# Attention products of a hybrid block: plain fp32 products rewritten as three passes over rounded halves

## The chip, the cores and the metric

The kernel runs on one core of one Trainium2 chip. The metric is the device time of one execution in microseconds (us), and the kernel before takes 2869.97 us, the median of 3 runs (2869.61 to 2870.84). Engines are named as in the profile: PE is TensorE with its weight loads PEld, DVE is VectorE, ACT is ScalarE, POOL is GpSimd, SP issues most DMAs.

## The reference

One recurrent and attention block is followed by two further layers, all on 256 tokens of width 2048 in fp32. What matters here are the three kinds of attention. Each head multiplies queries by keys (scores) and weights by values (weighted sums):

```python
# first block: 16 heads, "stick breaking", strictly causal
z = einsum('bhqd,bhkd->bhqk', qb, kb) * scale
w = where(causal, exp(log_sigmoid(z) + excl), 0.0)   # excl: suffix sums of log_sigmoid(-z)
out = einsum('bhqk,bhkd->bhqd', w, vb)
# two layers, 4 differential heads: two softmaxes over half the head width each
s = einsum('bqhcd,bkhcd->bhcqk', qi, k) * scale + bias
a = p[:, :, 0] - lam * p[:, :, 1];  out = einsum('bhqk,bkhd->bqhd', a, v)
# two layers, 8 dilated heads: a softmax over scores with bias, then the weighted sum
```

The rest are projections by large weight matrices (7852 blocks of 128x128, streamed from memory), a recurrence, a convolution of 31 taps in each of the two layers, norms and a feed-forward stage.

## The kernel before

Activations lie transposed, features on the 128 partitions and 256 tokens along the columns. Weights come in slabs of 8 blocks (`prep`, L196): a DMA brings `raw`, ACT writes the rounded high half `whi` (type fp32r), DVE writes the low half `wlo = raw - whi`. Four slabs are prepared ahead (`LA`). An activation is kept as a high and a low half side by side in one tile of 512 columns (`split`, L308). A projection (`proj`) runs, per block, a pass of the high weights over both halves (512 columns, L217) and a pass of the low weights over the high half (256 columns, L218). Where the output is narrower, `mm3` runs three passes of 256 columns (L220 to L222). Values are made by `vproj` with the tokens on the partitions.

The attention products were left as plain fp32 products: one of 256 columns and one of 128 columns for each score tile and for each weighted sum, since the upper right of the causal square is left out. Scores of the first block stand at L598 and L599, its weighted sums at L619 and L620. For both layers the scores stand at L795 and L796 (`scores`) and the weighted sums at L819 and L820 (`weighted`). The suffix sums of the first block are already products of halves with triangles and columns of minus one (`sum2`, L573 and L574).

PE runs in the order in which the program is written (`manual_schedule`). The attention steps are closures in a queue, `sides`: `interleave` cuts each head into stages, two steps apart, and `side()` runs one step behind every projection, or behind every fourth block in `vproj`. So the work of a head fills the gaps of the next projections. The instructions of ACT, DVE, POOL and SP are put in order by a list scheduler that goes by the program's order, moved up where `tc.high_priority()` stands. Each engine then runs its list strictly in order. The convolution taps (`tap`, L909, 31 for each of 4 column groups and each layer) run on DVE in the same stretch as the differential heads; `bg(n)` places them.

A softmax for the layers (`softmax`, `scale_rows`) is a chain on DVE, ACT and DVE: scores plus bias, row maximum, exponential with sum, reciprocal, scaling (L778 to L791). `transposed` sends its result through PE (L810 to L812) and ACT copies it out of PSUM. Tiles come from fixed sets: 51 slots `c` of 512 columns, 14 slots `w` of 384 columns, 4 PSUM tiles `pm`, 2 `pa` and 2 `pst`.

Of the kernel before, what the change touches and what calls it, by code (L numbers as in the profile page):

```python
# [13 lines left out]
OP = mybir.AluOpType  # L14
# [62 lines left out]
def hybrid_kernel(ctx, tc, wst, xin, pin, vec, cst, relb, onehot, out, order):  # L77
# [203 lines left out]
    def vproj(key, mc, ops, scale_cols, sides_between=True):  # L281
        os = [pm(512) for _ in range(2)]
        for kr, a in enumerate(ops):
            ah, al = hl(a)
            wh, wl = wnext(key, kr, mc, 4)
            first, last = kr == 0, kr == len(ops) - 1
            for b, o in enumerate(os):
                tb = slice(b * 128, (b + 1) * 128)
                PE.matmul(o, ah[:, tb], wh, start=first, stop=False)  # L289
                PE.matmul(o, ah[:, tb], wl, start=False, stop=False)  # L290
                PE.matmul(o, al[:, tb], wh, start=False, stop=last)  # L291
            if sides_between and kr % 4 == 3:
                side()
        v = []
        for b, o in enumerate(os):
            t = slot()
            if scale_cols is None:
                act(t, o, AF.Copy)
            else:
                act(t, o, AF.Copy, scale=scale_cols[:, b:b + 1])  # L300
            v.append([t[:, j * 128:(j + 1) * 128] for j in range(4)])
        return v

    def split(src):
# [271 lines left out]
    def head_job(col, gcol):  # L576
        o = proj("w_in", col, ops)
        q = joined(o, "qk", R)
        s = ct()
        with tc.high_priority():  # L580
            act(s, q, AF.Square)
            s = pool_split(s, *hl(slot(F32R)))

        def fin():
            p = pst()
            sum2(p[:, :256], ones1r, s)
            r = rsqrt(p[:, :256], EPS, ct(), ct())
            V.scalar_tensor_tensor(q, q, gcol, r, op0=OP.mult, op1=OP.mult)
        return q, fin

    yo = {}

    def stick_stages(h, q, k, v0, v1):
        d = {}

        def s1():
            p = pa()
            PE.matmul(p[:, 0:256], k[:, 0:128], q, start=True, stop=True)  # L598
            PE.matmul(p[:, 256:384], k[:, 128:256], q[:, 128:256], start=True, stop=True)  # L599
            z, t = wt(), wt()  # L600
            V.tensor_tensor(z, p[:, :384], maskneg, op=OP.add)
            act(t, z, AF.Abs)
            act(t, t, AF.Exp, scale=-1.0)
            act(t, t, AF.Ln, bias=one)
            V.scalar_tensor_tensor(t, z, 0.0, t, op0=OP.max, op1=OP.add)
            d["z"], d["t"] = z, pool_split(t, wt(384, F32R), wt(384, F32R))

        def s2():
            p = pa()
            t, z = d["t"], d["z"]  # L610
            sum2(p[:, 0:384], negtrir, t, last=False)
            sum2(p[:, 128:256], negonesr, [a[:, 256:384] for a in t], first=False)
            V.tensor_tensor(z, p[:, :384], z, op=OP.add)
            act(z, z, AF.Exp)

        def s3():
            p = pa()
            w = d["z"]
            PE.matmul(p[:, 0:256], v0, w[:, 0:256], start=True, stop=False)  # L619
            PE.matmul(p[:, 128:256], v1, w[:, 256:384], start=False, stop=True)  # L620
            yo[h] = split(p[:, 0:256])
            d.clear()
        return s1, s2, s3
# [168 lines left out]

    def scores(q, k):
        p = pa()
        PE.matmul(p[:, 0:256], q[:, 128:256], k, start=True, stop=True)  # L795
        PE.matmul(p[:, 256:384], q[:, 0:128], k[:, 0:128], start=True, stop=True)  # L796
        return p

    def apart(t):
        w = slot()  # L800
        a, b = hl(w)
        nc.gpsimd.memset(a[64:128], 0.0)
        nc.gpsimd.memset(b[0:64], 0.0)
        act(a[0:64], t[0:64], AF.Copy)
        act(b[64:128], t[64:128], AF.Copy)
        return w

    def transposed(s):
        p = pa()
        PE.transpose(p[:, 0:128], s[:, 256:384], ident)  # L810
        PE.transpose(p[:, 128:256], s[:, 0:128], ident)
        PE.transpose(p[:, 256:384], s[:, 128:256], ident)  # L812
        w = wt()
        act(w, p[:, :384], AF.Copy)
        return w

    def weighted(w, v0, v1):
        p = pa()
        PE.matmul(p[:, 0:256], v0, w[:, 0:256], start=True, stop=False)  # L819
        PE.matmul(p[:, 128:256], v1, w[:, 256:384], start=False, stop=True)  # L820
        return p[:, 0:256]

    def dil_stages(h, q, k, v0, v1, res):
# [16 lines left out]
    def diff_stages(h, q, k, v0, v1, nlam, gcol, res):  # L840
        d = {}

        def s1():
            d["a"], l = softmax(scores(q[:, 0:256], k), h, 64.0 ** -0.5)
            scale_rows(d["a"], l)

        def s1b():
            s, l = softmax(scores(q[:, 256:512], k), h, 64.0 ** -0.5)
            a = d["a"]
            V.tensor_tensor(l, l, nlam.to_broadcast([128, 2]), op=OP.mult)  # L850
            V.scalar_tensor_tensor(a[:, 0:256], s[:, 0:256], l[:, 0:1], a[:, 0:256], op0=OP.mult, op1=OP.add)
            V.scalar_tensor_tensor(a[:, 256:384], s[:, 256:384], l[:, 1:2], a[:, 256:384], op0=OP.mult, op1=OP.add)

        def s2():
            d["w"] = transposed(d.pop("a"))

        def s3():
            o = weighted(d.pop("w"), v0, v1)
            t, s = ct("resa"), ct()
            act(t, o, AF.Copy)  # L860
            act(s, o, AF.Square)
            d["t"], d["s"] = t, pool_split(s, *hl(slot(F32R)))

        def s4():
            t = d.pop("t")
            p = pst()
            sum2(p[:, :256], ones1r, d.pop("s"))
            r = rsqrt(p[:, :256], EPS_2, ct(), ct())
            V.scalar_tensor_tensor(t, t, gcol, r, op0=OP.mult, op1=OP.mult)
            res[h] = t  # L870
        return s1, s1b, s2, s3, s4

    for layer in range(DEPTH_2):
# [65 lines left out]
        def plain(col, key):  # L939
            return joined(proj(W, col, ops), key)  # L940

        aq, ak = [], []
        for lst, col in ((aq, C2_AQ), (ak, C2_AK)):
            for j in range(A_H):
                if layer and lst is aq:
                    t, b = folded(proj(W, col + j, dgs, cols=258), "aqk")
                    act(t, t, AF.Identity, bias=b)
                else:
                    t = plain(col + j, "aqk")
                lst.append(apart(t) if lst is aq else t)  # L950
                bg(4)
        if layer:
            del dgs
# [31 lines left out]
        for g in range(2):  # L985
            bq, bk = [], []
            for lst, col in ((bq, C2_BQ), (bk, C2_BK)):
                for j in range(4):
                    lst.append(plain(col + 4 * g + j, "bqk"))
                    bg(5 if g == 0 else 4)  # L990
                    side()
            bv = vproj(W, C2_BV + 4 * g, ops, None)
# [279 lines left out]
```

## Time and profile before

| what | us |
|---|---|
| median of 3 runs | 2869.97 |
| the profiled execution, its own time | 2869.06 |
| span of the profile, first to last instruction | 2866.9 |
| PE busy | 2846.1 (99%) |
| DVE busy | 2018.1 (70%) |
| ACT busy | 1645.0 (57%) |
| POOL busy | 136.8 (5%) |

The profiled execution took 0.91 us less than the median. The TensorE clock was granted in full (0.998 over the run). The lengths of matmuls in the profile overlap, since they are pipelined, so the cost of one is read from the distance between starts. On DVE, too, one instruction starts a little before the one ahead of it ends. A plain fp32 product appears as two matmul records and two weight loads, a product of rounded halves as one of each.

### The profile page before, as it was taken

Reading aid. Unit: us, or ns where it says so; the run is one execution under the profiler, and the core shown is the slowest. Engines: PE = TensorE matmul, PEld = TensorE weight load, DVE = VectorE, ACT = ScalarE, POOL = GpSimd, SP = SyncE. Lnnn points to the kernel's source line nnn. Section 1 sums busy time; section 2 is a strip of 40 time slices with the busy share of each in tenths; the row PEclk is TensorE's granted clock in tenths of the full one; section 3 lists DMA queues with packets and bytes.
Section 4 is the critical chain, followed back from the end, with each engine's and each line's share of the span. In section 5 each row is a group of like instructions: output and inputs, shape, how many; then the busy total and the mean of one; then the engine's idle time right before and its main releaser. Section 6 shows DMA issues by size and latency. Waiting matters only on the chain.

```text
span 2866.9 us, 43239 instructions
## 1 busy us (share of the span) xinstructions
PE 2846.1 (99%) x16414; PEld 2496.8 (87%) x16414; DVE 2018.1 (70%) x3306; ACT 1645.0 (57%) x2628; POOL 136.8 (5%) x155
## 2 busy tenths in 40 slices
PE   9999999999999999999999999999999999999997
PEld 8988888888888888888888888888888889888886
DVE  8788765666665776566565666776795688896676
ACT  6778764677765555544445455555464656554654
POOL 0112100111110000000000000000000001000000
PEclk9999999999999999999999999999999999999999
DMA  7565555545455556555555555655555555545553
GB/s 250 179 199 180 196 190 185 184 165 166 163 175 180 188 191 217 188 187 191 186 189 189 190 190 185 211 186 191 177 169 169 176 189 173 193 158 176 170 185 124
DMA packets 146433, 527.04 MB, mean 184 GB/s; under 512 B 16708, under 2 KB 17244, under 8 KB 146224
## 3 DMA queue, kind: packets, MB, share of 16 engines
q1 hardware_dynamic: 144720, 520.00, 54.8%
q0 software_dynamic: 1504, 4.29, 0.4%
q8 instruction: 128, 2.10, 0.3%
q14 instruction: 81, 0.66, 0.1%
HBM read 522.10 MB, written 4.47 MB: 184 GB/s over the span
## 4 chain that ended last, share of the span: by engine, by line
PE 99%; DVE 1%; DMA 0%; ACT 0%; SPq 0%; issue 0%; DVEq 0%
PE pm L217 55%; PE pm L218 28%; PE pm L290 3%; PE pm L289 3%; PE pm L291 3%; PE pm L221 2%; PE pm L220 2%; PE pm L222 2%; PE pa L795 0%; PE pa L819 0%; PE pa L598 0%; PE pa L796 0%; PE pa L619 0%; DVE x L1122 0%; DMA x<-xin_dram 0%; PE pa L217 0%
## 5 line engine op out<-in xcount | busy, mean ns | idle before, releaser
L217 PE MATMUL pm<-c,whi 128*128 128x512 f32 x6778 | 2382.6, 395 | 1.6 <-DVE c L355 1.6
L218 PE MATMUL pm<-c,wlo 128*128 128x256 f32 x6778 | 1898.5, 280 | 0.1
L196 DVE TENSOR_TENSOR wlo<-raw,whi 128x1024 fp32r<-128x1024 f32 (+1 forms) x984 | 1203.8, 1224 | 783.3 <-ACT whi L98 777.4
L98 ACT ACTIVATE whi<-raw 128x1024 fp32r<-128x1024 f32 (+1 forms) x984 | 1039.4, 1057 | 967.4 <-PE pm L217 500.4
L217 PEld LDWEIGHTS pm<-c,whi 128*128 128x128 f32 x6778 | 1273.1, 188 | 294.5 <-DVE c L355 1.9
L218 PEld LDWEIGHTS pm<-c,wlo 128*128 128x128 f32 x6778 | 1275.6, 188 | 0.8 <-DVE wlo L196 0.4
L98 ACT ACTIVATE c<-pm 128x256 f32<-128x256 f32 (+1 forms) x376 | 150.5, 402 | 110.7 <-PE pm L218 106.4
L98 ACT ACTIVATE c<-c 128x256 fp32r<-128x256 f32 (+2 forms) x357 | 139.2, 408 | 46.6 <-DVE c L450 24.9
L228 DVE TENSOR_TENSOR c<-pm,c 128x256 f32<-128x256 f32 x338 | 141.1, 418 | 4.5 <-ACT c L98 4.5
L289 PE MATMUL pm<-whi,c 128*128 128x512 f32 x320 | 126.9, 396 | 0.0
L290 PE MATMUL pm<-wlo,c 128*128 128x512 f32 x320 | 126.3, 395 | 0.0
L291 PE MATMUL pm<-whi,c 128*128 128x512 f32 x320 | 126.1, 394 | 0.0
L909 DVE SCALAR_TENSOR_TENSOR c<-w,sv,c 128x256 f32<-128x256 f32 x240 | 109.4, 497 | 0.8
L221 PE MATMUL pm<-c,whi 128*128 128x256 f32 (+1 forms) x377 | 106.4, 282 | 0.0
L220 PE MATMUL pm<-c,whi 128*128 128x256 f32 (+1 forms) x377 | 106.3, 282 | 0.0
L222 PE MATMUL pm<-c,wlo 128*128 128x256 f32 (+1 forms) x377 | 106.0, 281 | 0.0
L104 ACT ACTIVATE c<-c 128x256 f32<-128x256 f32 x219 | 85.5, 407 | 16.0 <-DVE c L228 14.1
L230 DVE TENSOR_TENSOR c<-c,c 128x256 f32<-128x256 f32 x176 | 75.8, 431 | 4.2
L291 PEld LDWEIGHTS pm<-whi,c 128*128 128x128 f32 x320 | 60.1, 188 | 14.2
L289 PEld LDWEIGHTS pm<-whi,c 128*128 128x128 f32 x320 | 60.1, 188 | 13.7
L290 PEld LDWEIGHTS pm<-wlo,c 128*128 128x128 f32 x320 | 60.1, 188 | 13.5
L220 PEld LDWEIGHTS pm<-c,whi 128*128 128x128 f32 x377 | 70.9, 188 | 0.9
(245 smaller groups left out, 1570.5 us busy)
## 6 DMA issues: line engine op xcount, KB each, us to landing
raw<-wst_dram SPq DMA_DIRECT2D x980, 512.0 KB, 3.3
scratch<-rows POOLq DMA_DIRECT2D x1, 2304.0 KB, 17.7
out_dram<-x SPq DMA_DIRECT2D x8, 256.0 KB, 2.0
x<-xin_dram SPq DMA_DIRECT2D x6, 256.0 KB, 7.7
c<-scratch POOLq DMA_DIRECT2D x12, 128.0 KB, 3.8
raw<-wst_dram SPq DMA_DIRECT2D x4, 256.0 KB, 4.0
sv<-vec_dram SPq DMA_DIRECT2D x1, 538.0 KB, 9.0
x<-xin_dram SPq DMA_DIRECT2D x4, 128.0 KB, 3.8
```

The costliest lines, as they stand in the source:

```text
L98: return S.activation(o, i, func, **kw)
L196: V.tensor_tensor(lo[:, s], raw[:, s], h[:, s].bitcast(F32), op=OP.subtract)
L217: PE.matmul(o, wh, a[:, 0:512], start=first, stop=False)
L218: PE.matmul(o[:, 256:512], wl, a[:, 0:256], start=False, stop=last)
L220: PE.matmul(o, wh, a[:, 0:n], start=first, stop=False)
L221: PE.matmul(o, wh, a[:, n:2 * n], start=False, stop=False)
L222: PE.matmul(o, wl, a[:, 0:n], start=False, stop=last)
L228: V.tensor_tensor(t, o[:, 0:256], t, op=OP.add)
L289: PE.matmul(o, ah[:, tb], wh, start=first, stop=False)
L290: PE.matmul(o, ah[:, tb], wl, start=False, stop=False)
L291: PE.matmul(o, al[:, tb], wh, start=False, stop=last)
L909: V.scalar_tensor_tensor(a, pad[:, k:k + 256], wcol, a, op0=OP.mult, op1=OP.add)
```

## The change

All queries, keys, values and attention weights are split into a rounded high half and a low half, and each plain fp32 product becomes three passes: high by high, high by low, low by high (`mm3c`). The splits are an ACT copy and a DVE subtraction each: of 256 columns for each query and key (72 times, in `head_job`, for the keys of the differential heads, and for queries and keys of the dilated heads), of 512 columns for each half of the values of a `vproj` and for each masked query tile of the differential heads (`half_split`, 28 times), and of 384 columns for the attention weights (`wsplit`, 40 times). In the two layers the ACT half of `wsplit` takes the place of the copy out of PSUM in `transposed`; in the first block it is added behind the exponential. Nothing else is changed; the numbers of slots stay.

```diff
@@ vproj
-            v.append([t[:, j * 128:(j + 1) * 128] for j in range(4)])
+            t = half_split(t)
+            v.append([cut(t, j) for j in range(4)])
@@ head_job, in fin
             V.scalar_tensor_tensor(q, q, gcol, r, op0=OP.mult, op1=OP.mult)
-        return q, fin
+            done.append(split(q))
+        return done, fin
+    def mm3c(o, w, a, to, frm, first=True, last=True):
+        (wh, wl), (ah, al) = w, a
+        PE.matmul(o[:, to], wh, ah[:, frm], start=first, stop=False)
+        PE.matmul(o[:, to], wh, al[:, frm], start=False, stop=False)
+        PE.matmul(o[:, to], wl, ah[:, frm], start=False, stop=last)
+    def cut(t, h):
+        return [a[:, h * 128:(h + 1) * 128] for a in t]
+    def half_split(t):
+        h, lo = slot(F32R), slot(F32R)
+        act(h, t, AF.Copy)
+        V.tensor_tensor(lo, t, h.bitcast(F32), op=OP.subtract)
+        return h, lo
+    def wsplit(s, E):
+        h, lo = wt(384, F32R), wt(384, F32R)
+        act(h, s, AF.Copy)
+        E.tensor_tensor(lo, s, h.bitcast(F32), op=OP.subtract)
+        return h, lo
@@ stick_stages
-            PE.matmul(p[:, 0:256], k[:, 0:128], q, start=True, stop=True)
-            PE.matmul(p[:, 256:384], k[:, 128:256], q[:, 128:256], start=True, stop=True)
+            kk, qq = hl(k[0]), hl(q[0])
+            mm3c(p, cut(kk, 0), qq, ALL, ALL)
+            mm3c(p, cut(kk, 1), qq, slice(256, 384), LATE)
             act(z, z, AF.Exp)
+            d["w"] = wsplit(z, V)
-            w = d["z"]
-            PE.matmul(p[:, 0:256], v0, w[:, 0:256], start=True, stop=False)
-            PE.matmul(p[:, 128:256], v1, w[:, 256:384], start=False, stop=True)
+            w = d["w"]
+            mm3c(p, v0, w, ALL, ALL, last=False)
+            mm3c(p, v1, w, LATE, slice(256, 384), first=False)
@@ scores, apart, transposed, weighted
-        PE.matmul(p[:, 0:256], q[:, 128:256], k, start=True, stop=True)
-        PE.matmul(p[:, 256:384], q[:, 0:128], k[:, 0:128], start=True, stop=True)
+        mm3c(p, cut(q, 1), k, ALL, ALL)
+        mm3c(p, cut(q, 0), k, slice(256, 384), slice(0, 128))
-        return w
+        h, lo = half_split(w)
+        return (h[:, 0:256], lo[:, 0:256]), (h[:, 256:512], lo[:, 256:512])
-        w = wt()
-        act(w, p[:, :384], AF.Copy)
-        return w
+        return wsplit(p[:, :384], V)
-        PE.matmul(p[:, 0:256], v0, w[:, 0:256], start=True, stop=False)
-        PE.matmul(p[:, 128:256], v1, w[:, 256:384], start=False, stop=True)
+        mm3c(p, v0, w, ALL, ALL, last=False)
+        mm3c(p, v1, w, LATE, slice(256, 384), first=False)
@@ keys of the differential heads; queries and keys of the dilated heads
-                lst.append(apart(t) if lst is aq else t)
+                lst.append(apart(t) if lst is aq else hl(split(t)))
-                    lst.append(plain(col + 4 * g + j, "bqk"))
+                    lst.append(hl(split(plain(col + 4 * g + j, "bqk"))))
```

The first place in the order is on PE, at the first scores of the first block; before, two plain products stand between two projections (pa is the score tile, c the halves of keys and queries):

```order
L218 MATMUL pm_6070<-c_290,wlo_6017 128x256
L598 MATMUL pa_6124<-c_5452,c_5687 128x256
L599 MATMUL pa_6124<-c_5452,c_5687 128x128
L217 MATMUL pm_6138<-c_110,whi_6016 128x512
L218 MATMUL pm_6138<-c_110,wlo_6017 128x256
```

and in the changed kernel, where L596 to L598 are the lines of `mm3c`:

```order
L218 MATMUL pm_6102<-c_290,wlo_6035 128x256
L596 MATMUL pa_6156<-c_5579,c_5847 128x256
L597 MATMUL pa_6156<-c_5579,c_5847 128x256
L598 MATMUL pa_6156<-c_5579,c_5847 128x256
L596 MATMUL pa_6156<-c_5579,c_5847 128x128
L597 MATMUL pa_6156<-c_5579,c_5847 128x128
L598 MATMUL pa_6156<-c_5579,c_5847 128x128
L217 MATMUL pm_6174<-c_110,whi_6034 128x512
```

Six instructions stand where two stood, at the same place among the projections.

The second place is on DVE in layer 0, at the softmaxes of the first two dilated heads. Before, the first head's weights w_20563 are scaled (L790, L791) ahead of the second head's scores w_20630 (L778):

```order
L786 RECIPROCAL s_20567<-s_20567 128x2
L909 SCALAR_TENSOR_TENSOR c_18987<-w_19084,sv,c_18987 128x256
L790 TENSOR_SCALAR w_20563<-w_20563,s_20567 128x256
L791 TENSOR_SCALAR w_20563<-w_20563,s_20567 128x128
L909 SCALAR_TENSOR_TENSOR c_18987<-w_19084,sv,c_18987 128x256
L196 TENSOR_TENSOR wlo_20610<-raw_20607,whi_20609 128x1024
L228 TENSOR_TENSOR c_20553<-pm_20576,c_20553 128x256
L778 SCALAR_TENSOR_TENSOR w_20630<-pa_20627,c_18072 128x256
```

In the changed kernel the same head is w_21014, the second w_21088, the scaling is at L817 and L818, and L309 is the subtraction of a query's split:

```order
L806 SCALAR_TENSOR_TENSOR w_21088<-pa_21081,c_18392 128x128
L808 TENSOR_REDUCE s_21091<-w_21088 128x1
L809 TENSOR_REDUCE s_21091<-w_21088 128x1
L813 RECIPROCAL s_21018<-s_21018 128x2
L309 TENSOR_TENSOR c_21074<-c_20997,c_21074 128x256
L810 TENSOR_SCALAR s_21091<-s_21091 128x2
L817 TENSOR_SCALAR w_21014<-w_21014,s_21018 128x256
L196 TENSOR_TENSOR wlo_21113<-raw_21110,whi_21112 128x1024
L813 RECIPROCAL s_21092<-s_21092 128x2
L818 TENSOR_SCALAR w_21014<-w_21014,s_21018 128x128
L817 TENSOR_SCALAR w_21088<-w_21088,s_21092 128x256
```

The scaling of the first head has moved behind the second head's scores and behind a slab of low weights; the PE transposes that read it keep their place.

## Rows read from the trace of the kernel before

**Rows 1.** The page, part 1: busy us (share of the span), times instructions, of each engine

```profile
PE 2846.1 (99%) x16414; PEld 2496.8 (87%) x16414; DVE 2018.1 (70%) x3306; ACT 1645.0 (57%) x2628; POOL 136.8 (5%) x155
```

**Rows 2.** The waits of PE: us in total, times, longest; the longest

```profile
PE pst L337 <- DVE c L384: 1.8, 1, 1.8
```

**Rows 3.** Groups by line and form: count, busy us, mean ns, idle before, its releaser

```profile
L795 PE MATMUL pa<-c,c 128*128 128x256 f32 x64 | 19.0, 379 | 0.0
L819 PE MATMUL pa<-w,c 128*128 128x256 f32 x48 | 14.2, 378 | 0.0
L598 PE MATMUL pa<-c,c 128*128 128x256 f32 x32 | 9.9, 392 | 0.0
L619 PE MATMUL pa<-w,c 128*128 128x256 f32 x32 | 9.5, 379 | 0.0
```

**Rows 4.** PE in order of time, two plain fp32 score products: start us, length us

```profile
2072.36 0.59 PE L795 MATMUL pa<-c,c 128*128 128x256 f32 x2
2072.79 0.38 PE L796 MATMUL pa<-c,c 128*128 128x128 f32 x2
2073.01 0.60 PE L795 MATMUL pa<-c,c 128*128 128x256 f32 x2
```

**Rows 5.** PE in order of time, three passes of 256 columns each

```profile
56.26 0.28 PE L220 MATMUL pm<-c,whi 128*128 128x256 f32 x1
...
56.61 0.28 PE L220 MATMUL pm<-c,whi 128*128 128x256 f32 x1
```

**Rows 6.** PE in order of time, two rounded passes of 128 columns, then plain ones

```profile
606.91 0.22 PE L573 MATMUL pa<-w,negonesr 128*128 128x128 f32 x1
606.98 0.27 PE L574 MATMUL pa<-w,negonesr 128*128 128x128 f32 x1
607.09 0.65 PE L598 MATMUL pa<-c,c 128*128 128x256 f32 x2
607.57 0.38 PE L599 MATMUL pa<-c,c 128*128 128x128 f32 x2
```

**Rows 7.** Groups by form: the weight loads of repeated weights

```profile
L221 PEld LDWEIGHTS pm<-c,whi 128*128 128x128 f32 x377 | 71.2, 189 | 0.0
```

**Rows 8.** Groups by form: subtractions on DVE

```profile
L196 DVE TENSOR_TENSOR wlo<-raw,whi 128x1024 fp32r<-128x1024 f32 x980 | 1201.1, 1226 | 779.6 <-ACT whi L98 773.8 <-PE pm L217 2.9 <-PE pm L218 2.3
L308 DVE TENSOR_TENSOR c<-c,c 128x256 fp32r<-128x256 f32 x146 | 58.7, 419 | 0.5 <-ACT c L98 0.5
L613 DVE TENSOR_TENSOR w<-pa,w 128x384 f32<-128x384 f32 x16 | 8.8, 548 | 0.0
```

**Rows 9.** DVE in order of time, two neighbours at 2132.6

```profile
2132.64 0.42 DVE L228 TENSOR_TENSOR c<-pm,c 128x256 f32<-128x256 f32 x1
2132.97 0.41 DVE L778 SCALAR_TENSOR_TENSOR w<-pa,c 128x256 f32<-128x256 f32 x1
```

**Rows 10.** Three stretches: us, then PE, PEld, DVE, ACT, POOL busy, clock, DMA

```profile
590.00:870.00 280.00, 280.00 (x1543) 243.15 (x1542) 187.20 (x295) 200.90 (x379) 48.19 (x43) 1.00 0.50 165
2053.00:2142.50 89.50, 89.50 (x494) 77.62 (x493) 85.02 (x197) 54.18 (x112) 3.26 (x4) 1.00 0.49 164
2509.00:2602.00 93.00, 93.00 (x514) 80.63 (x513) 86.78 (x199) 56.01 (x115) 3.21 (x4) 1.00 0.50 166
```

**Rows 11.** DVE: the end of a softmax of the dilated heads, layers 0 and 1

```profile
2136.73 0.28 DVE L791 TENSOR_SCALAR w<-w,s 128x128 f32<-128x128 f32 x1
2594.90 0.28 DVE L791 TENSOR_SCALAR w<-w,s 128x128 f32<-128x128 f32 x1
```

**Rows 12.** PE: the transposes that read these

```profile
2142.55 0.27 PE L810 MATMUL pa<-cs,w 128*128 128x128 f32 x1
2600.83 0.27 PE L810 MATMUL pa<-cs,w 128*128 128x128 f32 x1
```

**Rows 13.** POOL: the low half of a softplus; PE: the pass that reads it

```profile
621.60 1.65 POOL L569 TENSOR_TENSOR w<-w,w 128x384 fp32r<-128x384 f32 x1 [3.75 <-ACT w L98]
628.56 0.34 PE L574 MATMUL pa<-w,negtrir 128*128 128x384 f32 x1
```

More of the change, by code (lines that the diff above doesn't have):

```diff
@@ L578, in head_job @@
         q = joined(o, "qk", R)
+        done = []
         s = ct()
@@ L588, in fin @@
             V.scalar_tensor_tensor(q, q, gcol, r, op0=OP.mult, op1=OP.mult)
-        return q, fin
+            done.append(split(q))
[17 more added lines that the diff above has]
+        return h, lo
+    ALL, LATE = slice(0, 256), slice(128, 256)
     yo = {}
@@ L843, in s1 @@
         def s1():
-            d["a"], l = softmax(scores(q[:, 0:256], k), h, 64.0 ** -0.5)
+            d["a"], l = softmax(scores(q[0], k), h, 64.0 ** -0.5)
             scale_rows(d["a"], l)
         def s1b():
-            s, l = softmax(scores(q[:, 256:512], k), h, 64.0 ** -0.5)
+            s, l = softmax(scores(q[1], k), h, 64.0 ** -0.5)
             a = d["a"]
```

## Prediction

> **What bounds the kernel now.** I read the busy times first, then the waits of PE, then the price of one attention product, then the stretches in which DVE is full. PE is busy for 99% of the span [rows 1], and its longest wait is 1.8 us [rows 2]. The time is PE's own list of passes, run back to back. A change pays if the list becomes shorter, and costs if it becomes longer or if something that PE reads comes late. DVE at 70% and ACT at 57% [rows 1] have room on average; the reader should not trust the average, since the change adds work to stretches where DVE has next to none.
>
> **How many products are touched.** A plain product leaves two matmul records, so 64, 48, 32 and 32 records [rows 3] are 32, 24, 16 and 16 products of 256 columns: 88, each with a partner of 128 columns behind it.
>
> **Before.** Lengths of pipelined matmuls overlap, so I take starts. Two score pairs stand back to back: 2072.36, 2072.79, then the next pair at 2073.01 [rows 4]. A pair takes 0.65 us: 0.43 for 256 columns, 0.22 for 128. Over 88 pairs that is 57 us.
>
> **After.** Each pair becomes three passes of 256 and three of 128 columns. Three rounded passes of 256 columns run from 56.26 to 56.61 [rows 5], 0.117 us each. Rounded passes of 128 columns occur in the suffix sums: two of them start at 606.91 and 606.98 and the next product at 607.09, 0.18 us for both; but that product then needs 0.48 us to its successor (607.09 to 607.57) where it otherwise needs 0.43 [rows 4, 6]. So the two take 0.23 us, 0.11 to 0.115 each, nearly as much as 256 columns. I take 0.11. A pair is then 3 x 0.117 + 3 x 0.11 = 0.68 us against 0.65: 0.033 us longer, and 88 x 0.033 = 2.9 us in all. Rounding saves on the wide product, and at 128 columns it gives the saving back. Bounds: narrow passes at 0.09, the 0.18 without what the next product loses, give a pair of 0.62 and -2.6 us; at 0.117, like wide ones, 0.70 and +4.6 us. The high weights serve two passes running, but the second pass of this pattern has a load of its own 377 times [rows 7], so nothing is saved there.
>
> On the narrow pass a page disagrees with the row. The Trainium skill, "TensorE: Matmul & The Clock Gate", section "Back-to-back issue gap", gives about 81 ns for one matmul of 128 columns in a stream of loads and matmuls. By it a pair would be an estimated 0.59 us, and the products would gain 5 us instead of losing 2.9. The row measures 0.11 and has the type, size and neighbours of this kernel, so it decides here.
>
> **The splits.** The change adds 140 subtractions on DVE: 72 of 256 columns, 40 of 384, 28 of 512. Their lengths are 419 and 548 ns, and about 690 ns for 512 columns (an estimate on the line between 419 and 1226 ns) [rows 8]. DVE starts an instruction before the last has ended: one of 0.42 us is followed 0.33 us later [rows 9], so each costs 0.085 less. That is 72 x 0.335 + 40 x 0.465 + 28 x 0.605 = 60 us on DVE. ACT gets 116 copies, some 48 us at the same lengths. Where the engines have room I price both at nothing: in the first block DVE and ACT leave about a third and a quarter of the time free, and PE's passes hide the work [rows 10]. One chain there is shortened. POOL writes the low half of a softplus from 621.60 to 623.25, and PE reads it at 628.56 [rows 13], 5.3 us of lead. It waits for ACT, and each head puts three to four copies of about 0.4 us on ACT, 1.5 us. I leave it at 0, with 1 us in each of the four groups of heads as the upper bound, for two heads' copies and POOL's own 1.65 us falling together.
>
> **The place without room.** While the differential heads of a layer run, DVE also runs the convolution taps. From the first differential scores to the first transposes of a dilated head (2053.0 to 2142.5) DVE is busy 85.0 of 89.5 us, ACT 54.2; layer 1 is alike, 86.8 of 93 [rows 10]. Into the first stretch the new order puts 10 subtractions of 256, 4 of 384 and 2 of 512 columns: 3.4 + 1.9 + 1.2 = 6.4 us, more than the 4.5 us that are free, while PE lengthens the stretch only by 14 pairs x 0.033 = 0.5 us. What is late next: the scaled weights of the first dilated head. Before, they are done at 2137.01 and PE wants them at 2142.55; in layer 1 at 2595.18 and 2600.83: leads of 5.5 and 5.7 us [rows 11, 12]. A demand 6.4 us larger eats that lead and leaves 6.4 - 0.5 - 5.5 = 0.4 us of lateness. Behind the transposes on PE stand all later projections, so lateness is PE idle time and is not given back. The new order also moves this scaling behind the second head's scores, two maxima and a slab of low weights, some 2.5 us at the lengths of rows 8; with all of it the lateness would be 2.9 us, with the exponential on ACT and the hand-overs 3.5. Against that the list can put off taps, and part of the free 4.5 us lies where the added work can use it; then nothing is late. I take 1.3 us for each layer, between 0 and 3.5 and nearer to the plain difference. Two layers: 2.6 us, from 0 to 7.
>
> **The sum.** 2869.06 of the profiled execution + 2.9 for the products + 2.6 for the waits = 2874.6 us. The profiled execution stood 0.91 us under the median, so the median of the changed kernel should be near 2875 us, 0.18% above 2869.97.
>
> **Rivals.**
> - DVE becomes the bound in both stretches (slower). It decides once DVE's backlog at a dilated head's scores exceeds the 3 us or so of work between them and the scaling: then the second head's softmax is late like the first. For it: 85.0 + 6.4 is more than 89.5 [rows 10]. Against: the taps end near there, and the list was made with the added work in it. Price 3.5 us, or with a second late head 2.5 us more, 6 for each layer; with the 2.9 that is 2879 to 2884 us.
> - A narrow pass costs only its columns (faster). Half of a wide pass's 0.117 is 0.06, and one such distance between starts is seen, 606.91 to 606.98 [rows 6]. A pair is then 0.53 us, 88 x -0.12 = -10.3 us: 2861 us with the waits. Against: the time comes back in the next two starts of the same rows.
> - Narrow passes overlap partly with their neighbours. Midway between 0.06 and 0.11 a pair is 0.61 us, 88 x -0.044 = -3.9 us: 2868 us with the waits. Rows 6 hold one pair of narrow passes and can't exclude it for three running.
> - The change does not do what it says: if the rounded halves ran like plain fp32, a pair would be 3 x 0.65 and the kernel 114 us slower. The suffix sums show such tiles in single records [rows 6], so I give it nothing.
>
> **How the numbers follow.** What a measurement of this kernel can tell from no change is about 0.2%, 5.7 us. My forecast, a small loss on PE and short waits, has 0.62, and its own range, 2867 to 2879, crosses that line: 0.40 within it, 0.22 above. DVE as the bound has 0.22, all slower. The narrow pass at its columns has 0.09, all faster; partly overlapped 0.07, no change. Together: faster 0.09, same 0.47, slower 0.44. The range goes from 2864, between the two cheaper cases, to 2885, the sum of the upper bounds: 2869.06 + 4.6 + 7 + 4 for the first block's chain.
>
> **What would show it.** The wide passes of a pair should start 0.117 apart and the narrow ones cost 0.11, with 0.68 us for a pair; 0.53 or 0.61 would make the product term wrong. DVE should be above 95% in the two stretches, and the only new waits of PE should be those of the transposes for DVE, one or two for each layer and near 1 us. Waits spread over more heads would mean the slower rival; none, that the list gave way. The time would be wrong if PE waited in the first block, or if projections waited for low weights.

## Result: 0.6% slower, and where the time went

The changed kernel takes 2888.14 us (median of 6 runs, 2883.69 to 2888.83) against 2870.4 us (2869.28 to 2871.54) for the kernel before: 17.7 us more, a ratio of 1.006 with the interval 1.0049 to 1.007. The forecast was 2875, its range 2864 to 2885. The profiled execution took 2886.24 us with a span of 2884.5, against 2869.06 and 2866.9. The spread of the changed kernel goes with the TensorE clock granted over a whole run: 0.998 at 2883.69 us, 0.997 in the profiled execution, 0.996 in the four runs at 2888.0 and above.

The page's busy times, which answer to [rows 1]:

```profile
PE 2856.3 (99%) x16590; PEld 2508.6 (87%) x16590; DVE 2088.4 (72%) x3446; ACT 1692.1 (59%) x2744; POOL 133.9 (5%) x155
```

PE still shows 99%. DVE has 70 us more where the forecast had 60, ACT 47 where it had 48. The share hides what happened; the waits of PE show it (us in total, times, longest). Before, the longest was 1.8 us [rows 2]; now three kinds stand ahead of it:

```profile
PE pa L838 <- DVE w L818: 3.7, 2, 1.9
PE pa L574 <- DVE w L627: 2.1, 3, 0.7
PE pa L574 <- DVE c L309: 2.0, 3, 0.7
```

To see what each place costs in all, I compared starts: PE reads the same slabs of weights in the same order in every kernel here, so the start of the first pass that reads a slab is a milestone. The stretches are named by the trace before, the kernels as in the experiments below. Each row is the profiled execution of one kernel, each number its length less that of before, in us:

| kernel | start to 573 | first block, 573 to 944 | 944 to 2068 | both layers, 2068 to 2789 | rest |
|---|---|---|---|---|---|
| changed | +0.33 | +6.53 | +0.81 | +9.94 | -0.07 |
| stick_only | +0.66 | +6.58 | +0.69 | +1.97 | +0.20 |
| layers_only | +0.91 | 0.00 | +0.11 | +7.69 | -0.15 |
| pm | +0.34 | +4.42 | +0.81 | +8.44 | -0.07 |
| taps | +1.62 | +6.56 | +0.81 | +2.87 | -0.22 |
| pm_taps | +0.58 | +4.42 | +0.81 | +2.88 | -0.22 |
| splits_only | +0.20 | +4.36 | +3.59 | +1.72 | +0.07 |
| zpool | +0.48 | +3.99 | +0.81 | +2.87 | -0.22 |
| shift1 | -0.13 | +5.94 | +0.48 | +2.21 | -0.22 |
| yocopy_taps | +0.19 | +4.01 | -0.14 | +3.63 | -0.15 |
| narrow_taps | +1.81 | +2.79 | +1.42 | -2.58 | +0.04 |
| narrow_taps_zpool | -0.13 | +2.86 | +1.42 | -2.58 | +0.04 |
| narrow_taps_yocopy | +1.45 | -2.22 | +0.46 | -2.65 | +0.41 |

Every kernel, the one before too, has a wait of 1.76 us near 40 us. In layers_only, taps, narrow_taps and narrow_taps_yocopy the granted clock falls to its lower level behind it, and their start is 0.9 to 1.8 us longer; in the other traces it does not fall, and the start is within -0.1 and +0.7. So the first column says nothing about the edits. The changed kernel loses 6.5 us in the first block and 9.9 us in the layers.

**The passes.** PE in order of time, two score pairs back to back, which answer to [rows 4]:

```profile
2080.06 0.28 PE L596 MATMUL pa<-c,c 128*128 128x256 f32 x1
2080.18 0.28 PE L597 MATMUL pa<-c,c 128*128 128x256 f32 x1
2080.29 0.28 PE L598 MATMUL pa<-c,c 128*128 128x256 f32 x1
2080.41 0.22 PE L596 MATMUL pa<-c,c 128*128 128x128 f32 x1
2080.47 0.27 PE L597 MATMUL pa<-c,c 128*128 128x128 f32 x1
2080.58 0.28 PE L598 MATMUL pa<-c,c 128*128 128x128 f32 x1
2080.69 0.33 PE L596 MATMUL pa<-c,c 128*128 128x256 f32 x1
2080.86 0.28 PE L597 MATMUL pa<-c,c 128*128 128x256 f32 x1
```

Wide passes start 0.11 to 0.12 apart, narrow ones 0.06, 0.11 and 0.11. A pair takes 0.63 us, and the first pass behind it 0.17 in place of 0.12: 0.68, as forecast. Of the 48 score pairs, 38 stand in front of a projection. From the first start of such a pair to the second start behind it there are 0.93 us in the median, against 0.89 before; added up over all 88 pairs, without the waits, the difference is about 2.9 us, the term of the forecast.

**The first block.** PE in order of time while the second head group is projected (in brackets: idle before, releaser), then DVE and ACT in the same microseconds:

```profile
629.65 0.27 PE L598 MATMUL pa<-w,c 128*128 128x128 f32 x1
630.60 0.45 PE L574 MATMUL pa<-w,negtrir 128*128 128x384 f32 x1 [0.67 <-DVE c L309]
```

```profile
627.94 1.23 DVE L196 TENSOR_TENSOR wlo<-raw,whi 128x1024 fp32r<-128x1024 f32 x1
629.09 1.12 DVE L612 TENSOR_TENSOR w<-w,w 128x384 fp32r<-128x384 f32 x1
630.13 0.41 DVE L309 TENSOR_TENSOR c<-pa,c 128x256 fp32r<-128x256 f32 x1
```

```profile
628.16 0.51 ACT L98 ACTIVATE w<-w 128x384 fp32r<-128x384 f32 x1
...
628.88 0.36 ACT L98 ACTIVATE c<-pa 128x256 fp32r<-128x256 f32 x1
```

The softplus pass L574 starts 0.95 us behind the last product. Its own data are there (POOL ended their low half at 627.52); what it lacks is a PSUM bank. The pool pa has two, and the one that is due still holds the previous head's weighted sum, which ACT copies at 628.88 and DVE reads last, from 630.13 to 630.54 (L309). The weighted sum had been complete since about 622. New in front of these readers are the weights' copy on ACT (628.16) and their low half on DVE (L612). In the kernel before, the same reader is done at 626.99, 1.3 us ahead of the pass that needs the bank:

```profile
625.42 1.23 DVE L196 TENSOR_TENSOR wlo<-raw,whi 128x1024 fp32r<-128x1024 f32 x1 [0.69 <-ACT whi L98]
626.57 0.42 DVE L308 TENSOR_TENSOR c<-pa,c 128x256 fp32r<-128x256 f32 x1
```

```profile
628.30 0.42 PE L573 MATMUL pa<-w,negtrir 128*128 128x384 f32 x1
```

There are six such waits, two in each of three head groups; for three of them the late reader is the mask addition (L627). The slabs behind them start 0.9 to 1.0 us later each.

**The layers.** DVE at the first dilated head of layer 0, the counterpart of [rows 11], and PE in the same place:

```profile
2150.83 0.34 DVE L817 TENSOR_SCALAR w<-w,s 128x256 f32<-128x256 f32 x1
2151.09 1.22 DVE L196 TENSOR_TENSOR wlo<-raw,whi 128x1024 fp32r<-128x1024 f32 x1
...
2152.30 0.26 DVE L818 TENSOR_SCALAR w<-w,s 128x128 f32<-128x128 f32 x1
```

```profile
2152.62 0.33 PE L838 MATMUL pa<-cs,w 128*128 128x128 f32 x1 [1.79 <-DVE w L818]
...
2156.31 0.63 PE L217 MATMUL pm<-c,whi 128*128 128x512 f32 x1
...
2156.95 0.44 PE L217 MATMUL pm<-c,whi 128*128 128x512 f32 x1
...
2157.35 0.39 PE L217 MATMUL pm<-c,whi 128*128 128x512 f32 x1
```

The lead of 5.5 us that the scaled weights had [rows 11, 12] is gone, and PE idles 1.79 us; in layer 1 it idles 1.92. A slab's low half (L196) even stands between the two halves of the scaling. From the first differential scores to these transposes DVE is busy 89.0 of 92.1 us, in layer 1 89.1 of 92.2: 97% in both, above the 95% that the prediction asked for. Then the projection's pairs of passes start 0.64 us apart (2156.31 to 2156.95) in place of some 0.35, which they are nearly back at with the next pair (0.40): the granted clock is at the lower of its two levels, 1.2 GHz, from 2153.6 to 2157.0, which costs some 1.5 us more. The windows around both places show it in the clock's column, with those of the kernel taps below them (us, then PE, PEld, DVE, ACT, POOL busy, clock, DMA):

```profile
2142.50:2165.00 22.50, 20.70 (x118) 18.14 (x117) 20.54 (x54) 13.93 (x31) 0.00 (x0) 0.92 0.48 165
2600.00:2625.00 25.00, 23.08 (x133) 20.24 (x131) 23.27 (x55) 13.44 (x30) 0.00 (x0) 0.93 0.54 182
```

```profile
2140.00:2162.00 22.00, 22.00 (x136) 19.58 (x136) 22.00 (x58) 13.39 (x28) 0.00 (x0) 1.00 0.50 162
2600.00:2625.00 25.00, 25.00 (x156) 22.31 (x155) 25.00 (x66) 15.58 (x34) 0.00 (x0) 1.00 0.49 165
```

The fall does not come with every wait. The kernel pm has the same two waits, of 1.82 and 1.92 us, and its clock falls behind the second only; this is its window around the first:

```profile
2140.00:2162.00 22.00, 20.18 (x124) 17.71 (x124) 21.50 (x54) 14.18 (x32) 0.00 (x0) 1.00 0.50 174
```

In layers_only, with waits of 1.97 and 2.01 us, it falls behind the first only. So the clock fell behind four of six such waits. By the starts around the first wait (2135 to 2150 in the trace before) the changed kernel takes 3.67 us more than the kernel before, pm 2.15, and taps, which has no wait there, 0.14: 2.0 us for the wait and 1.5 for the fall.

### The profile page after: what moved, and what is told of

Same layout as the page of the kernel before. It is cut to its first block, busy times and chain, and to the rows that moved or that the text cites. A ratio compares the mean times of both kernels' runs of the same rounds, so it can differ in the third digit from the quotient of the medians.

```text
span 2884.5 us, 43860 instructions
## 1 busy us (share of the span) xinstructions
PE 2856.3 (99%) x16590; PEld 2508.6 (87%) x16590; DVE 2088.4 (72%) x3446; ACT 1692.1 (59%) x2744; POOL 133.9 (5%) x155
## 4 chain that ended last, share of the span: by engine, by line
PE 94%; ACT 3%; DVE 2%; issue 1%; DMA 0%; SPq 0%; DVEq 0%; ACTq 0%
PE pm L217 52%; PE pm L218 26%; PE pm L289 3%; PE pm L291 3%; PE pm L290 3%; PE pm L221 2%; PE pm L220 2%; PE pm L222 2%; ACT whi L98 1%; DVE wlo L196 1%; ACT c L98 1%; PE pa L598 1%; PE pa L597 1%; PE pa L596 0%; ACT c L104 0%
## 5 line engine op out<-in xcount | busy, mean ns | idle before, releaser
L217 PE MATMUL pm<-c,whi 128*128 128x512 f32 x6778 | 2386.0, 395 | 1.7 <-DVE c L356 1.7
L196 DVE TENSOR_TENSOR wlo<-raw,whi 128x1024 fp32r<-128x1024 f32 (+1 forms) x984 | 1202.8, 1223 | 724.3 <-ACT whi L98 717.2
L217 PEld LDWEIGHTS pm<-c,whi 128*128 128x128 f32 x6778 | 1274.4, 188 | 296.5 <-DVE c L356 2.3
L98 ACT ACTIVATE c<-c 128x256 fp32r<-128x256 f32 (+3 forms) x457 | 186.6, 423 | 106.1 <-DVE c L228 43.8
L309 DVE TENSOR_TENSOR c<-c,c 128x256 fp32r<-128x256 f32 x218 | 89.5, 422 | 3.5 <-ACT c L98 3.2
```

Source lines behind the costliest of these rows:

```text
L98: return S.activation(o, i, func, **kw)
L196: V.tensor_tensor(lo[:, s], raw[:, s], h[:, s].bitcast(F32), op=OP.subtract)
L217: PE.matmul(o, wh, a[:, 0:512], start=first, stop=False)
```

## Experiments

Twelve kernels, each set against the kernel before as measured beside it: pm, taps, splits_only and pm_taps against 2869.6 us, stick_only, layers_only and the two with yocopy against 2869.57, the other four against 2869.92 (medians of 14 to 29 runs). "The table" is that of the result.

**pm: another bank for the weighted sum.**

```
         def s3():
-            p = pa()
+            p = pm()
```

> Only change to the changed kernel: in the first block the weighted sum of a head goes to a bank of the pool of four (pm) in place of the pool of two (pa); the order of DVE, ACT and PE stays. The trace of the changed kernel has six starts of the softplus pass (L574) that come 0.7 to 0.95 us after the product before it in place of 0.11, in the last two steps of three head groups. Theory A: each waits for its PSUM bank of the pair, whose last reader (the split of the weighted sum, L309, or the mask addition, L627) DVE does late because the new low-half subtraction stands ahead of it; with a bank of its own the six waits go, about 5.3 us: 2888 -> 2883 against 2870 for the kernel before (+12), and the profile has no wait of L574. Rival B: DVE itself is late and the bank is only where it shows; then the waits return at the sums' own data or at a bank of the four: 2887 to 2889 (+17).

Measured: 2882.73 us, ratio 1.0044 (1.0031 to 1.0057). The six waits of L574 are gone, but the value projection now waits for the same reader:

```profile
PE pm L289 <- DVE c L309: 2.5, 3, 0.9
```

The median is A's number, but by luck. The first block gains 2.1 us by the table, not 5.3. Another 1.5 us lie in the layers, which the edit leaves alone, where the clock fell once in place of twice; and the changed kernel's median stands 1.9 us above its profiled execution. So the wait is for a bank, as A says, and another bank doesn't cure it, as B says: the reader itself is late, and whoever needs its bank next waits.

**taps: the convolution's taps later.**

```
-                bg(4)
+                bg(2)
...
-                    bg(5 if g == 0 else 4)
+                    bg(3 if g == 0 else 5)
```

> Only change to the changed kernel: the convolution taps of the two layers are handed out later (2 in place of 4 a projection of the first heads' queries and keys, 3 in place of 5 in the first dilated group, 5 in place of 4 in the second), so that some 65 in place of 118 taps of a layer stand on DVE ahead of the first dilated head's scaled weights. Theory A: the two waits of the dilated transposes (L838, 1.9 to 2.1 us each) come from DVE's backlog there, and each brings some 1.5 us more in which the granted clock is at half (0.91 and 0.95 in the 20 us windows around them); without the backlog both go, 7 us in all: 2888 -> 2881 (+11), no wait of L838, clock 1.00 in these windows. Rival B: the taps only hand the backlog on to the convolution's sum and norm, and PE waits there: no more than 3 us back, 2885 (+15). Rival C: the waits come from the chain itself and not from the queue: 2888.

Measured: 2879.79 us, ratio 1.0032 (1.0019 to 1.0044). No wait of L838 is left, the clock is 1.00 in the windows above, and the layers take 7.07 us less (9.94 - 2.87). Theory A holds. By the waits the two transposes idle 3.7 us; most of the rest was the slower clock behind them, which the changed kernel's trace has twice. Against pm, whose clock fell once, the same edit gives 5.56 us (8.44 - 2.88, under pm_taps).

**splits_only: the splits without the passes.**

```
-            mm3c(p, cut(kk, 0), qq, ALL, ALL)
-            mm3c(p, cut(kk, 1), qq, slice(256, 384), LATE)
+            PE.matmul(p[:, 0:256], k[0][:, 0:128], q[0], start=True, stop=True)
+            PE.matmul(p[:, 256:384], k[0][:, 128:256], q[0][:, 128:256], start=True, stop=True)
...
```

> All splits into high and low halves are still made, as in the changed kernel, but nothing reads them: the 88 pairs of products are the plain fp32 ones of before. Theory A: the passes cost little (0.02 to 0.03 us a pair, 2 to 3 us in all) and the splits' work on DVE and ACT costs the rest by waits: 2884 to 2886 against 2870 (+14 to +16), with the waits of L574 and L838 still there. Rival B: the three passes themselves cost it, in loads of weights or at the engine's change between kinds of product: 2870 to 2872 (0 to +2).

Since nothing reads the splits, the plain copy of the transposed weights is back beside them: 24 copies on ACT more than in the changed kernel.

Measured: 2879.45 us, ratio 1.0033 (1.002 to 1.0045): a miss for both. Waits for the bank remain, three of them:

```profile
PE pa L574 <- DVE c L309: 3.3, 3, 1.1
```

The transposes don't wait, but only just. DVE, then PE, at the first dilated head of layer 0:

```profile
2150.73 0.48 DVE L819 TENSOR_SCALAR w<-w,s 128x128 f32<-128x128 f32 x2
```

```profile
2151.06 0.33 PE L839 MATMUL pa<-cs,w 128*128 128x128 f32 x1
```

The first of these two scalings ends near 2151.0, and the transpose that reads it starts at 2151.06. The lead of 5.5 us has gone here too, so the splits alone cause the backlog; whether it becomes a wait hangs on the last microsecond or two of DVE's order, which differs from that of the changed kernel. And 3.59 us were lost between 944 and 2068, where PE runs the same passes as before and waits for nothing; that is taken up under shift1.

**pm_taps: both edits.**

> Both edits together: bank of its own for the weighted sum of the first block, and the taps handed out later. Theory A: the two places are independent and both come from waits for DVE: 12.4 us back, 2888 -> 2875.5 against 2870 (+5), which leaves 2.9 us for the passes and some 2 us of small things. Rival B: most of the difference is spread over all products: 2880 to 2884.

Measured: 2877.24 us, ratio 1.0026 (1.0016 to 1.0036). The two edits add up in the table (first block +4.42 as in pm, layers +2.88 as in taps); A is 1.7 us too low; of the 5.3 us that it counted for the first block, 2.1 came.

**zpool: the weights' low half on POOL.** On top of taps:

```
-            d["w"] = wsplit(z, V)
+            d["w"] = wsplit(z, nc.gpsimd)
```

> The kernel with the taps handed out later, and one edit more: in the first block the low half of the stick weights (16 subtractions of 384 columns) is made by POOL in place of DVE. With the taps alone the time is 2879.8 (six waits of L574, 4.1 us by the table of waits). Theory A: the banks come free late because this subtraction (0.55 us, up to 1.1 beside a POOL operation) stands on DVE right ahead of their last readers (L309, L627); without it these are 0.6 to 1.1 us earlier and most of the wait goes: 2875 to 2876, waits of L574 under 1.5 us. Rival B: POOL's operations hold DVE up while they run (POOL 626.32 to 627.52 stands beside a DVE multiplication of 1.24 us that takes 0.41 elsewhere), so 16 more of them give the gain back: 2879 to 2881, waits of L574 or of others as long as before.

Measured: 2877.23 us, ratio 1.0027 (1.0017 to 1.0036). The waits fall from 4.1 to 1.6 us, the first block by 2.57 (6.56 - 3.99):

```profile
PE pa L574 <- DVE c L309: 0.9, 3, 0.3
PE pa L574 <- DVE w L627: 0.7, 3, 0.2
```

This subtraction ahead of the bank's readers makes a good half of the waits: theory A in mechanism, with 1.6 us left where it allowed 1.5 and a time 1 us above its range.

**narrow_taps: narrow products plain.** On top of taps; the splits that only they read go:

```
-            mm3c(p, cut(kk, 1), qq, slice(256, 384), LATE)
+            PE.matmul(p[:, 256:384], k[1][:, 128:256], q[1][:, 128:256], start=True, stop=True)
...
-        mm3c(p, cut(q, 0), k, slice(256, 384), slice(0, 128))
+        PE.matmul(p[:, 256:384], q[2][:, 0:128], k[2][:, 0:128], start=True, stop=True)
...
```

> The kernel with the taps handed out later, but of each of the 88 pairs only the 256-column product is made of three rounded passes; the 128-column one is a plain fp32 product, as before. Splits that only the narrow product read are left out (its halves of queries, keys, values and weights). Theory A: the narrow product in three passes is bound by its three loads (0.06 + 0.11 + 0.11, and the next instruction's), some 0.33 us, against 0.22 for the plain one; the pair falls from 0.68 to 0.57 us, 88 x 0.106 = 9.3 us: 2879.8 -> 2870.5, level with before, and shorter waits of L574, as DVE has less to do: down to 2868. Rival B: the change between rounded and plain passes costs 0.05 us or more each way, twice a pair: no more than 2 us back, 2878.

Measured: 2871.91 us, ratio 1.0005 (0.9997 to 1.0014). PE in order of time:

```profile
622.22 0.28 PE L601 MATMUL pa<-w,c 128*128 128x256 f32 x1
...
622.58 0.38 PE L652 MATMUL pa<-w,c 128*128 128x128 f32 x2
622.72 0.42 PE L578 MATMUL pa<-w,negtrir 128*128 128x384 f32 x1
622.98 0.34 PE L579 MATMUL pa<-w,negtrir 128*128 128x384 f32 x1
```

The pair takes 0.50 us, and L578 behind it 0.26. In front of a projection, by the same measure as above, a score pair takes 0.82 us in the median, against 0.93 in the changed kernel and 0.89 before: 0.11 less for each of 88 pairs is some 9 us, as A says. The first block falls by 3.77 us and the layers by 5.45, together 9.2; the medians differ by 7.9 only, and 0.6 us were lost between 944 and 2068. A also hoped for shorter waits; there are three now in place of six, each twice as long:

```profile
PE pa L578 <- DVE c L313: 4.3, 3, 1.4
```

ACT at one of them, and PE:

```profile
629.60 0.36 ACT L98 ACTIVATE c<-pm 128x256 f32<-128x256 f32 x1
...
630.17 0.37 ACT L98 ACTIVATE c<-pa 128x256 fp32r<-128x256 f32 x1
```

```profile
631.37 0.45 PE L578 MATMUL pa<-w,negtrir 128*128 128x384 f32 x1 [1.41 <-DVE c L313]
```

The weighted sum was complete at about 623, but its copy stands on ACT behind the copy of a later projection (c<-pm). The bank is late by the order on ACT as well as on DVE.

**narrow_taps_zpool.**

> All three: taps later, narrow products plain, the low half of the stick weights (256 columns) on POOL. Theory A (the costs are the passes of the narrow products and DVE's queue in the first block, and they add up): 2870.5 - 4 = 2866.5, 3 us under before (2869.6). Rival B (POOL holds DVE up, or the change of kinds costs): 2870 to 2876, not under before.

Measured: 2872.1 us, ratio 1.0006 (0.9997 to 1.0015), no gain on narrow_taps; its wait is the same 4.3 us. With narrower splits the low half of the weights isn't what keeps the bank. Theory A fails here, and the time is in B's range; but the waits are no longer than without POOL's part, so B's contention is not what the trace shows. The weighted sum's copy stands late on ACT, and the last run shows what an earlier one does.

**shift1: the ring one place on.** On top of taps:

```
+    V.memset(slot(), 0.0)
     mix = []
```

> The kernel with the taps handed out later and one memset of a tile of the ring of 51 more, ahead of the first block's output projection: all later tiles of the ring lie one place further. No product, split or order is changed. In the stretch between the first block and the layers (slabs 320 to 680, from 944 to 2068 in the kernel before), where PE waits for nothing, the traces took 1124.0 us before, 1124.8 in the changed kernel and in two variants that leave the ring as it is, and 1127.6 with the splits alone, whose ring stands elsewhere. Theory A: the place of a moving tile in the memory sets a few ns of its pass (226 to 238 ns for 512 columns, the same at each use): the stretch takes another time, 0.5 to 3 us off 1124.8, with no wait added. Rival B: it has another cause (the clock of that run, the instructions' fetch): 1124.8 within 0.1.

Measured: 2879.45 us, ratio 1.0034 (1.0022 to 1.0045). The stretch 944 to 2068 took 1124.47 us in place of 1124.80: 0.33 less. That is off 1124.80 by more than B allows, but under the half microsecond that A named. The place of tiles in the ring does move the time of unchanged passes; that it makes the whole 3.59 us of splits_only is not shown.

The first block shows something that the edit did not aim at. Five waits of L574 are left in place of six, though the added tile comes behind them and DVE's order is that of taps. At the head without a wait, the weights' low half (L612) took 0.55 us; at the two others of its kind it took 1.13 and 1.14, as it takes 1.12 at all three in the changed kernel. There POOL's subtraction beside it took 0.74 us; here it is POOL's that is long (DVE, POOL, then PE):

```profile
707.20 0.55 DVE L612 TENSOR_TENSOR w<-w,w 128x384 fp32r<-128x384 f32 x1
```

```profile
707.18 1.16 POOL L570 TENSOR_TENSOR c<-c,c 128x256 fp32r<-128x256 f32 x1 [1.53 <-ACT c L98]
```

```profile
708.14 0.44 PE L574 MATMUL pa<-w,negtrir 128*128 128x384 f32 x1
```

L574 starts 0.36 us behind the last product, in place of 0.95. So at such a head over half a microsecond of the lateness is the new subtraction's extra length beside POOL, and it can stay away where nothing in front of it was changed.

**stick_only and layers_only: one part each.** The other part as in the kernel before:

> One part of the change alone: three passes in the first block (32 pairs), the two layers as before. Theory A (the differences are local and add up): six waits of L574 with what they hide, 5.5 us by the starts of the slabs in the changed kernel's trace, and 32 x 0.033 = 1.1 us of passes: 2870 -> 2876.5 (+6 to +7). Rival B (what happens in one block shifts the rest, or the difference is spread): +9 to +12, or under +4.

> The other part alone: three passes in the two layers (56 pairs), the first block as before. Theory A: two waits of the dilated transposes with the slow clock after them, 7.3 us, 56 x 0.033 = 1.8 us of passes and about 1 us from the ring's new places: 2870 -> 2880 (+9 to +11); with the part above the sum is +16 to +18. Rival B: as above, the two parts do not add up to +17.7 within 2 us.

Measured: 2878.85 us, ratio 1.0032 (1.002 to 1.0045), and 2877.85 us, ratio 1.0028 (1.0017 to 1.004): +9.3 and +8.3, together +17.6 for the +17.7 of both. Their waits (of stick_only, then of layers_only):

```profile
PE pa L577 <- DVE w L630: 2.1, 3, 0.7
...
PE pa L577 <- DVE c L312: 2.0, 3, 0.7
```

```profile
PE pa L839 <- DVE w L819: 4.0, 2, 2.0
```

Each part brings its own waits, and they add up, as A says; that they do so to 0.1 us is partly luck. stick_only is 2 to 3 us above A's forecast, in B's range: 2.66 us came in stretches whose instructions are those of before (0.69 and 1.97 in the table). layers_only is 0.7 us below its forecast; in its trace the clock fell behind one wait, where the forecast had counted two.

**yocopy_taps: the bank emptied by ACT at once.** On top of taps:

```
-            yo[h] = split(p[:, 0:256])
+            t = ct()
+            with tc.high_priority():
+                act(t, p[:, 0:256], AF.Copy)
+            yo[h] = split(t)
```

> The kernel with the taps handed out later; in the first block ACT copies each weighted sum out of its PSUM bank at high priority, and the split is made from the copy (one ACT copy of 256 columns more a head, 16 of 0.41 us; the copy stands right behind an earlier projection's copy on ACT, some 3 us ahead of where the split's copy stood). Theory A: three of the six waits of L574 are for the bank that this split held (L309, 2.0 us by the table) and go; the three for the mask addition (L627, 2.1 us) stay: 2879.8 -> 2877 (+7). Rival B: DVE's and ACT's backlog shows at another place: 2879.5.

Measured: 2877.41 us, ratio 1.0026 (1.0015 to 1.0037). The waits for L309 are gone, those for L627 (2.1 us) stay; the first block falls by 2.55 us. As A said.

**narrow_taps_yocopy: a version that beats both.**

> Narrow products plain, taps later, and the weighted sum copied out of its bank by ACT at high priority. With narrow products plain and taps later the time is 2871.9, and its trace has one kind of wait that the kernel before lacks: three of L578 for the bank that the split of the weighted sum holds, 4.3 us, 1.4 each (starts 1.79 us apart in place of 0.14). Theory A: the bank comes free some 3 us earlier and all three go: 2871.9 -> 2867, 3 us under the kernel before (2869.9). Rival B: another wait takes their place: 2870 to 2872.

Measured: 2865.63 us (2864.66 to 2866.79), ratio 0.9987 (0.9978 to 0.9996): 3.9 us under the kernel before, 1.4 under A's number, and 22.5 under the changed kernel. At 0.82 us a pair in place of 0.89 the 88 pairs alone would be some 6 us faster than before; where the other 2 went is open. The three waits for the bank are gone, and the longest wait of PE is the one of 1.8 us that the kernel before has too [rows 2].

The bank is free at 627.23, and the next head's weighted sum, which stands ahead of the pass that needs it, begins at 628.86 (ACT, then PE):

```profile
626.86 0.37 ACT L98 ACTIVATE c<-pa 128x256 f32<-128x256 f32 x1
```

```profile
628.86 0.28 PE L601 MATMUL pa<-w,c 128*128 128x256 f32 x1
```

## Why the prediction was wrong, step by step

- **The number of products, their price before and after: right.** 0.68 us a pair came out as worked, and of the three prices for a narrow pass the row's 0.11 held. The starts around all pairs give 2.9 us, and in the first block 6.53 us less some 5.5 for the waits leave 1.0 for 32 pairs, 0.03 each. The cheaper rivals fall, and so does the estimate of 0.59 us a pair.
- **"Where the engines have room I price both at nothing", the first block: this step failed.** It cost some 5.5 us (the starts behind the six waits are 0.9 to 0.95 us later each), above the bound of 4. The engines do have room, as the stretch of [rows 10] shows in the changed kernel (DVE 214 of 280 us, ACT 215), and the chain that was examined, POOL's low half of the softplus, kept a lead of 3.2 us or more at every head, where it had 4.3 or more before. PE's own column is 4 us short of 280:

```profile
590.00:870.00 280.00, 275.94 (x1566) 240.69 (x1565) 214.44 (x335) 215.29 (x420) 43.87 (x43) 1.00 0.49 160
```

  What became late was a reader that frees a PSUM bank: the same pass L574 needs its data and an empty bank, and only the data were checked. The bank's lead before was 1.3 us, and the row stood in the trace. At the head shown two things eat it. The slab's low half in front of the reader starts 1.85 us before the pass is due, where it was 2.88 before; and the new subtraction puts 1.04 us between the two, half of it because POOL runs beside it.
- **The place without room: right in place and mechanism, its size too small.** The waits are those of the transposes, one in each layer, and splits_only shows the lead gone without any of the new passes. Forecast 1.3 us each; PE idled 1.8 to 1.9 us and lost 2.0 by the starts, inside the bounds. What the sum had no term for is the clock behind the wait, 1.5 us where it fell: twice in the changed kernel's trace, once in those of pm and layers_only. That is 7.1 us in place of 2.6 by the first, just above the upper bound of 7, and 5.6 by pm. The traces don't show why it fell behind one wait and not behind another.
- **The rival of a bound DVE (2879 to 2884)** named the right engine, and DVE was as full as it said, but its second late head did not come: each layer has one wait.
- **The rest.** First block and layers lost 6.5 + 9.9 us, and the named terms explain 5.5 + 7.1 + 2.9. The remaining microsecond, and the 0.8 between 944 and 2068, where but for four score pairs no pass changed, had no term. A tile's place in the ring moves such passes; how far it explains them stays open. The last 1.9 us, from the profiled execution to the median, go with the lower clock of the other runs.
- Of what would show the forecast wrong, "PE waited in the first block" came true.

## What to carry to other kernels

When work is added to an engine that frees buffers, check for each pass of the bound engine two leads: that of its data, and that of the bank or buffer that it writes; the smaller one is the room, whatever the engine's busy share. A forecast wait of PE near 2 us should be priced as a range, without and with slow passes behind it; here that was 2.0 or 3.5 us. Before two profiled executions are compared, look whether the clock fell equally often in both. Narrow products lost by rounded halves here (0.33 us for three passes against 0.22 plain), wide ones gained (0.35 against 0.43): of a pair, split only the wide product.

## What the runs showed of the hardware

- **A short wait can cost twice, but need not.** After 1.79 us of idleness the granted clock fell from 2.4 to 1.2 GHz about a microsecond after PE had begun again, and the passes ran at half speed until 2157.0 (rows of L217 above), which cost 1.5 us. It fell behind four of the six waits of 1.8 to 2.0 us in the layers (changed, pm, layers_only), and behind the 1.76 us near 40 us in four of the fourteen traces. Behind the waits of 0.7 us in the first block, and of 1.4 us in narrow_taps, it did not fall.
- **DVE is slow beside POOL.** A multiplication of two tiles in the changed kernel takes three times as long while POOL runs; DVE, then POOL:

```profile
626.23 0.41 DVE L309 TENSOR_TENSOR c<-c,c 128x256 fp32r<-128x256 f32 x1
626.56 1.24 DVE L230 TENSOR_TENSOR c<-c,c 128x256 f32<-128x256 f32 x1
```

```profile
626.32 1.20 POOL L570 TENSOR_TENSOR w<-w,w 128x384 fp32r<-128x384 f32 x1 [6.55 <-issue]
```

  The Trainium skill, "SBUF — State Buffer", section "Who interferes with whom", says that a DVE instruction with two inputs in SBUF contends with a GpSimd instruction that reads SBUF; this trace agrees, 1.24 us against 0.41. L612, ahead of the bank's reader, is 1.12 us long in place of 0.55 where POOL runs beside it; at the one head of shift1 it was POOL that took longer, 1.16 us in place of 0.74.
- **Unchanged passes do not take the same time in every kernel.** Between 944 and 2068 PE runs the same passes in all kernels, but for four score pairs at the end, and waits for nothing. It took 1123.8 to 1127.6 us from kernel to kernel, while the changed kernel, pm, taps and zpool, whose ring is the same there, agree at 1124.80. One tile more in the ring moved it by 0.33 us.
